# Eight modulation units earlier, another pass order, and a layernorm written out by hand in a two-layer diffusion trunk

## The chip, the cores and the metric

One core of a Trainium2 chip runs the whole program. The metric is the device time of one execution in microseconds; the median of the runs counts. TensorE (PE) does the matrix products, VectorE (DVE), ScalarE (ACT) and GpSimd (POOL) the elementwise work, and SyncE's queue (SP) issues the loads.

## The reference

A latent stream x of 512 tokens and 1024 features goes through two layers, with 256 context tokens beside it that the first layer's attention reads. Layer 0 mixes by grouped attention of 16 heads over 4 key and value heads, layer 1 by a Conformer convolution module, and each ends with a squared-ReLU feed-forward stage of 4096. All of it is in 32 bit floats.

```python
sh1, sc1, g1, sh2, sc2, g2 = split(silu(c) @ mod_w[i] + mod_b[i], 6)     # modulation of layer i
h = rms_norm(x, norm1_g[i]) * (1 + sc1) + sh1
y = dense_gqa(h, hc) if i == 0 else conformer_conv(h)
x = x + g1 * y
h = rms_norm(x, norm2_g[i]) * (1 + sc2) + sh2
x = x + g2 * (square(relu(h @ mlp_up[i])) @ mlp_down[i])

def conformer_conv(h):
    a, g = split(h @ w_pw1 + b_pw1, 2)
    u = a * sigmoid(g)
    u = depthwise_conv(u, w_dw, width=31) + b_dw
    u = silu(layer_norm(u, ln_g, ln_b))          # over the 1024 channels
    return u @ w_pw2 + b_pw2
```

## The kernel before

Features lie on the 128 partitions, in eight tiles of 128 x 512 (`x[j]`, the normed activations as high part `hh[j]` and low part `hl[j]`). A product of 32 bit floats is made of three matmuls: high weights by high activations, high weights by low activations, low weights by high activations (`passes`). Weights come in 1 MB loads (`raw`, two buffers). ACT casts the high part `whi` and DVE subtracts the low part `wlo` (`split_parts`, L418 and L423), in halves of 128 x 1024; for positions in `POOLW`, numbers of the list of weight loads, POOL subtracts. The pool for these parts is `whl`, or, for the up pairs of the later feed-forward stage, `extra[0]` (four buffers each).

The six modulation vectors of a layer are needed as columns. DVE makes them in 80 units (`mod_unit`, L654): one multiplies a load of 512 KB (`mraw`, two buffers) by a row and adds it up. `mod_run(k)` does the next k units and issues the load for two units ahead on SP, so a unit's load waits until the unit two places earlier is done. Units are strewn over the program as filling work: one or two in each head of the attention, `WOT` many around the halves of the projection behind it, eight behind the first up product of the feed-forward stage, more between its later products.

`pair_gemm` makes four output tiles in four PSUM banks, in two halves of 256 columns, `hf`. It is used in `proj_residual` (the attention's output and the convolution's second product, both with an evacuation on DVE for each bank and half that adds to x and takes the squares for the next norm), for the first up product, and for the first pointwise product of the convolution. `mlp` is the feed-forward stage: `relu2` squares on ACT (L705, L691, L692, the high part `ah`) and subtracts on DVE (L697, the low part `al`), then down products alternate with up products. At the end of layer 0's stage the last down product goes in two halves (L912) with the norm for layer 1 between them.

`conv(j)` makes the depthwise convolution of tile j as matmuls, evacuates it in 16 pieces of 32 x 128 (L1599 on ACT, L1596 on DVE), and `center` (L1619 to L1627) subtracts or adds an offset, squares on ACT and adds into the sums `ds_` and `qs`. Behind tile 7 two matmuls for each half sum over the partitions (L1673, L1674), ACT and DVE form the inverse deviation (`r0`), and for each tile DVE subtracts and scales (L1693, L1694), ACT applies silu and casts the high part (L1696, L1697), and POOL subtracts the low part `hl` (L1698). ACT's functions lie in tables that `act_set` loads (L390).

Outside of blocks named `manual_schedule`, the order on each engine is set by the framework's scheduler, which moves instructions past each other where data allow; inside them it is the order in which the code is written.

## Time and profile before

| | |
|---|---|
| median of three runs | 1283.16 us (1281.66 to 1286.63) |
| profiled execution | 1286.02 us, of which the span is 1284.0 |
| PE busy | 1227.1 us (96%) |
| DVE, ACT, POOL busy | 946.5 (74%), 693.7 (54%), 123.0 (10%) |
| chain that ended last | PE 78%, DVE 11%, issue 4%, ACT 4%, DMA 3% |
| granted clock, mean | 0.98 |

Matmuls overlap, so a busy PE is one that has a matmul under way. A row of the timeline gives the start, the time of its instructions together, engine, line, operation and tiles, and in brackets the idle time ahead of it on that engine with the instruction that ended it. The chain is followed back from the last instruction to whatever released it.

### The profile page before, as it was taken

What the parts mean: (1) busy time and instruction counts of PE and PEld (TensorE: products, weight loads), DVE (VectorE), ACT (ScalarE), POOL (GpSimd) and SP (SyncE); (2) the same over time, 40 slices, a digit from 0 to 9 for tenths busy, and PEclk for the clock granted to TensorE, in tenths of its full rate; (3) what the DMA queues carried; (4) which work ended last, traced back from release to release, by engine and by line L of the source; (5) the groups of instructions that cost most, each with busy time, mean ns of one, the idle gap of its engine ahead of it and who ended that gap; (6) DMA issues with size and microseconds to landing.
All of it is one profiled execution on the core that took longest, in us unless ns stands there. A gap on an engine that the chain in (4) does not pass through costs nothing.

```text
span 1284.0 us, 18207 instructions
## 1 busy us (share of the span) xinstructions
PE 1227.1 (96%) x6964; PEld 1042.8 (81%) x6964; DVE 946.5 (74%) x1665; ACT 693.7 (54%) x1297; POOL 123.0 (10%) x172
## 2 busy tenths in 40 slices
...
GB/s 347 158 70 85 31 63 66 67 97 108 217 115 267 180 214 163 164 181 128 168 148 148 165 133 172 181 124 1 132 67 66 91 107 99 99 99 100 102 96 65
DMA packets 36086, 163.08 MB, mean 127 GB/s; under 512 B 4000, under 2 KB 4384, under 8 KB 25120
## 3 DMA queue, kind: packets, MB, share of 16 engines
...
q8 instruction: 54, 0.88, 0.3%
...
## 4 chain that ended last, share of the span: by engine, by line
PE 78%; DVE 11%; issue 4%; ACT 4%; DMA 3%; POOL 0%; SPq 0%; DVEq 0%; ACTq 0%; POOLq 0%
PE sn L750 16%; PE mm L629 9%; PE mm L630 9%; PE mm L631 9%; PE pv L630 7%; PE pv L631 6%; PE pv L629 6%; PE pv L1429 4%; PE pv L1588 2%; PE sn L1369 2%; PE mm L1411 1%; PE mm L1410 1%; DVE wlo L423 1%; DMA mraw<-in_modt_dram 1%; DVE mlo L1015 1%
## 5 line engine op out<-in xcount | busy, mean ns | idle before, releaser
L418 ACT CAST whi<-raw 128x1024 fp32r<-128x1024 f32 x128 | 132.7, 1050 | 170.2 <-PE mm L630 62.0
L423 DVE TENSOR_TENSOR wlo<-raw,whi 128x1024 fp32r<-128x1024 f32 x124 | 150.8, 1223 | 56.0 <-ACT whi L418 53.4
L629 PE MATMUL mm<-hh,whi 128*128 128x256 f32 (+1 forms) x408 | 133.9, 329 | 0.0
L630 PE MATMUL mm<-hl,whi 128*128 128x256 f32 (+1 forms) x408 | 132.9, 326 | 0.0
L631 PE MATMUL mm<-hh,wlo 128*128 128x256 f32 (+1 forms) x408 | 132.9, 327 | 0.0
L629 PE MATMUL mm<-ah,whi 128*128 128x512 f32 (+1 forms) x324 | 123.0, 380 | 3.1 <-DVE x L912 3.1
L630 PE MATMUL mm<-al,whi 128*128 128x512 f32 (+1 forms) x324 | 123.1, 380 | 0.0
L631 PE MATMUL mm<-ah,wlo 128*128 128x512 f32 (+1 forms) x324 | 123.1, 380 | 0.0
L654 DVE SCALAR_TENSOR_TENSOR t<-mraw,sbc 128x1024 bf16<-128x1024 f32 x80 | 97.4, 1222 | 17.4 <-DMA mraw<-in_modt_dram 17.2
L454 DVE TENSOR_TENSOR wlo<-raw,whi 128x1024 fp32r<-128x1024 f32 (+1 forms) x80 | 86.9, 1087 | 12.5 <-ACT whi L446 12.3
L446 ACT CAST whi<-raw 128x1024 fp32r<-128x1024 f32 (+1 forms) x80 | 75.2, 941 | 34.7 <-DMA raw<-in_up_dram 15.6
L629 PE MATMUL pv<-hh,whi 128*128 128x256 f32 (+1 forms) x264 | 84.6, 321 | 9.7 <-ACT hh L1697 4.3
L750 PE MATMUL sn<-hh,wlo 128*128 128x256 f32 x320 | 89.7, 280 | 0.0
L750 PE MATMUL sn<-hl,whi 128*128 128x256 f32 x320 | 89.7, 280 | 0.0
L630 PE MATMUL pv<-al,whi 128*128 128x512 f32 (+1 forms) x224 | 86.1, 384 | 3.8 <-DVE al L697 3.8
L750 PE MATMUL sn<-hh,whi 128*128 128x256 f32 x320 | 89.6, 280 | 0.0
L797 DVE SCALAR_TENSOR_TENSOR x<-mm,mcol,x 128x512 f32<-128x512 f32 x65 | 48.7, 750 | 50.5 <-PE mm L631 50.5
L631 PE MATMUL pv<-ah,wlo 128*128 128x512 f32 (+1 forms) x224 | 85.7, 383 | 0.0
L629 PE MATMUL pv<-ah,whi 128*128 128x512 f32 (+1 forms) x224 | 85.6, 382 | 0.0
L630 PE MATMUL pv<-hl,whi 128*128 128x256 f32 (+1 forms) x264 | 84.2, 319 | 0.9 <-POOL hl L1698 0.9
L631 PE MATMUL pv<-hh,wlo 128*128 128x256 f32 (+1 forms) x264 | 84.3, 319 | 0.6 <-POOL wlo L423 0.6
L629 PEld LDWEIGHTS mm<-hh,whi 128*128 128x128 f32 x408 | 78.1, 192 | 7.3 <-ACT t L1641 0.4
...
## 6 DMA issues: line engine op xcount, KB each, us to landing
mraw<-in_modt_dram SPq DMA_DIRECT2D x80, 512.0 KB, 4.5
...
mraw<-in_modp_dram SPq DMA_DIRECT2D x10, 512.0 KB, 8.4
...
```

The source lines that it names most:

```text
L418: nc.scalar.copy(hi, raw[:, i * 1024:(i + 1) * 1024])
L423: eng.tensor_tensor(out=lo, in0=raw[:, i * 1024:(i + 1) * 1024], in1=hi.bitcast(F32), op=ALU.subtract)
L446: nc.scalar.copy(hi[:, :n], raw[:, o:o + n])
L454: nc.vector.tensor_tensor(out=lo[:, :n], in0=raw[:, o:o + n], in1=hi[:, :n].bitcast(F32), op=ALU.subtract)
L629: nc.tensor.matmul(acc, lhsT=ahi, rhs=bhi, start=first, stop=False)
L630: nc.tensor.matmul(acc, lhsT=ahi, rhs=blo, start=False, stop=False)
L631: nc.tensor.matmul(acc, lhsT=alo, rhs=bhi, start=False, stop=last)
L654: nc.vector.scalar_tensor_tensor(out=tmp(1024, mybir.dt.bfloat16), in0=raw, scalar=1.0, in1=sbc, op0=ALU.mult, op1=ALU.mult, accum_out=mco ...
L750: nc.tensor.matmul(acc, lhsT=a, rhs=b, start=first and k == 0 and i == 0, stop=k == 3 and i == 2, skip_group_check=not first)
L797: nc.vector.scalar_tensor_tensor(out=x[j], in0=acc, scalar=col(l, 5, j), in1=x[j], op0=ALU.mult, op1=ALU.add)
L1369: nc.tensor.matmul(sn[:, :384], lhsT=q1[:, tt * P:(tt + 1) * P], rhs=k1[kv][:, b * 384:(b + 1) * 384], start=True, stop=True)
L1429: nc.tensor.matmul(pv, lhsT=vt[:, f, i:i + P], rhs=p_, start=t == 0, stop=t == NKT - 1)
```

## The change

Six things are changed.

- `POOLW` is empty: the low parts of the second and third pointwise weight loads go from POOL to DVE.
- `WOT` becomes ((4, 4, 2), (3, 0, 0)), and the last three heads of the attention do a unit each; `mod_run(8)` behind the first up product is gone. So eight of the 80 units move: three into the attention, five into the projection.
- The last two down weights of layer 0 are split into the pool of the up pairs instead of `whl`.
- `pair_gemm` goes, for each k, through four matmuls of high by high, four of low weights, and four of low activations, instead of three for each bank in turn.
- The last two tiles of the convolution are evacuated half by DVE and half by ACT from two banks (`MERGED`); the table load for Ln and Exp moves to just behind the last sigmoid; the last tile enters the sums by matmuls that accumulate onto those of `ds_` and `qs`, without additions on DVE.
- The layernorm is written in a `manual_schedule` of DVE and ACT, in which scaling and subtracting alternate by tile and silu and cast too, and both halves' deviations are formed ahead of the silu table load.

```diff
--- before.py
+++ after.py
@@ -33,15 +33,15 @@
 NBLK = 7
 SHUF = 2
 OFFJ = 6
-LASTD = 3
+MERGED = {6: 2, 7: 2}
 KVCUT = [2, 3, 4]
 NU = 16
 KP = (0, 3)
 QP = (1, 0)
 RM = ((1, 1), (1, 1))
 SPLIT = (3,)
-POOLW = (43, 44)
-WOT = ((4, 4, 0), (0, 0, 0))
+POOLW = ()
+WOT = ((4, 4, 2), (3, 0, 0))
 FULL = [t for t in range(NKT) if t not in SPLIT]
 
 B0 = 1
@@ -504,7 +504,7 @@
                 wlist.append(up[l, g])
             else:
                 wlist.append(down[l, g, i[0]])
-        mlp_pos.append((start, set(ups)))
+        mlp_pos.append((start, set(ups + ([len(wlist) - 2, len(wlist) - 1] if l == 0 else []))))
 
     mlp_w(0)
     for i in range(8):
@@ -607,9 +607,14 @@
         for hf in range(2):
             hs = HS[hf]
             for k in range(NT):
-                for i in range(4):
-                    passes(accs[i][:, hs], *ws[i // 2](k * 256 + i % 2 * P, P), hh[k][:, hs], hl[k][:, hs],
-                           k == 0, k == NT - 1)
+                ops = [(accs[i][:, hs], *ws[i // 2](k * 256 + i % 2 * P, P)) for i in range(4)]
+                bhi, blo = hh[k][:, hs], hl[k][:, hs]
+                for acc, wh, _ in ops:
+                    nc.tensor.matmul(acc, lhsT=wh, rhs=bhi, start=k == 0, stop=False)
+                for acc, _, wl in ops:
+                    nc.tensor.matmul(acc, lhsT=wl, rhs=bhi, start=False, stop=False)
+                for acc, wh, _ in ops:
+                    nc.tensor.matmul(acc, lhsT=wh, rhs=blo, start=False, stop=k == NT - 1)
             if evac is not None:
                 for i in range(4):
                     evac(i, hf, accs[i][:, hs])
@@ -761,8 +766,6 @@
             extra[0], extra[1] = mp, ups
             proj_residual(l, v, norm_mlp(l, full))
             accs = pair_gemm(None, None)
-            if l == 0:
-                mod_run(8)
             for i in range(4):
                 relu2(mp, at, i, accs[i])
             t, quad, t1_split = quads(mp, full)
@@ -1502,7 +1505,7 @@
                 while tasks.get(g):
                     tasks[g].pop(0)()
                 if t == 2 and h < NH:
-                    mod_run(2 if h % 4 == 0 and h < 12 else 1 if h < 13 else 0)
+                    mod_run(2 if h % 4 == 0 and h < 12 else 1)
                 if g == NH * NKT - 12:
                     w_prefetch(1)
 
@@ -1573,8 +1576,8 @@
             cv = ps.tile([P, 512], F32, tag="pv", name="pv", bufs=2)
             last = j == NT - 1
             cvs = [cv] * NPH
-            if last:
-                cvs[LASTD:] = [mm_bank()] * (NPH - LASTD)
+            if j in MERGED:
+                cvs[MERGED[j]:] = [ps.tile([P, 512], F32, tag="mm", name="mm", bufs=3)] * (NPH - MERGED[j])
             zj = cp.tile([P, SEQ], F32, name=f"z{j}")
             off = None
             if j >= OFFJ:
@@ -1588,11 +1591,17 @@
                     nc.tensor.matmul(cvs[gq][:, gq * P:(gq + 1) * P], lhsT=tz[:, b], rhs=u[:, gq, b + B0:b + B0 + P],
                                      start=b == b0, stop=b == NBLK - 1)
             z.append(zj)
+            if last:
+                md.extend(sn_bank()[:, 0:256] for _ in range(2))
+                eq.extend((sn_bank()[:, 0:256], ps.tile([P, 512], F32, tag="mm", name="mm", bufs=3)[:, 0:256]))
+                for hf in range(2):
+                    nc.tensor.matmul(md[hf], lhsT=inv_d, rhs=ds_[:, HS[hf]], start=True, stop=False)
+                    nc.tensor.matmul(eq[hf], lhsT=inv_d, rhs=qs[:, HS[hf]], start=True, stop=False)
             for s in range(NPH):
                 for gq in range(4):
                     ch = slice(gq * 32, (gq + 1) * 32)
                     dst, src = zj[ch, s * P:(s + 1) * P], cvs[gq][s * 32:(s + 1) * 32, gq * P:(gq + 1) * P]
-                    if last and gq < LASTD:
+                    if gq < MERGED.get(j, 0):
                         nc.vector.scalar_tensor_tensor(out=dst, in0=src, scalar=pcol("bdw", j)[ch],
                                                        in1=off[ch, s * P:(s + 1) * P], op0=ALU.add, op1=ALU.add)
                     else:
@@ -1615,17 +1624,21 @@
             if off is None:
                 nc.vector.tensor_tensor(out=z[j][:, hs], in0=z[j][:, hs], in1=cb[:, hs], op=ALU.subtract)
             else:
-                ch = slice(LASTD * 32 if j == NT - 1 else 0, P)
+                ch = slice(MERGED[j] * 32, P)
                 nc.vector.tensor_tensor(out=z[j][ch, hs], in0=z[j][ch, hs], in1=off[ch, hs], op=ALU.add)
             s = tmp(256)
             nc.scalar.activation(s, z[j][:, hs], AF.Square)
             if j == 0:
                 nc.vector.tensor_copy(qs[:, hs], s)
                 nc.vector.tensor_copy(ds_[:, hs], z[j][:, hs])
+            elif j == NT - 1:
+                nc.tensor.matmul(md[hf], lhsT=inv_d, rhs=z[j][:, hs], start=False, stop=True)
+                nc.tensor.matmul(eq[hf], lhsT=inv_d, rhs=s, start=False, stop=True)
             else:
                 nc.vector.tensor_tensor(out=ds_[:, hs], in0=ds_[:, hs], in1=z[j][:, hs], op=ALU.add)
                 nc.vector.tensor_tensor(out=qs[:, hs], in0=qs[:, hs], in1=s, op=ALU.add)
 
+        md, eq = [], []
         for j in range(NT):
             if j == 0:
                 accs4 = pair_gemm(None, None)
@@ -1639,6 +1652,8 @@
                         passes(accs[m], *w(k * 256 + m * P, P), hh[k], hl[k], k == 0, k == NT - 1)
             sg = tmp()
             nc.scalar.activation(sg, accs[1], AF.Sigmoid, bias=pcol("bpw1", 8 + j))
+            if j == NT - 1:
+                act_set("natural_log_exp_and_others")
             u = cp.tile([P, 4, P + 8], F32, tag="u", name="u", bufs=3)
             nc.gpsimd.memset(u[:, :, 0:4], 0.0)
             nc.gpsimd.memset(u[:, :, P + 4:], 0.0)
@@ -1664,38 +1679,57 @@
                     center(i // 2, i % 2)
             if j:
                 conv(j - 1)
-        act_set("natural_log_exp_and_others")
         conv(NT - 1)
-        md, eq = sn_bank(), sn_bank()
-        rs = [None, None]
-        for hf in range(2):
+        var = [cp.tile([P, 256], F32, name=f"var{hf}") for hf in range(2)]
+        r0 = [cp.tile([P, 256], F32, name=f"r0_{hf}") for hf in range(2)]
+        ET = mybir.EngineType
+
+        def ln_var(hf):
             hs = HS[hf]
-            nc.tensor.matmul(md[:, hs], lhsT=inv_d, rhs=ds_[:, hs], start=True, stop=True)
-            nc.tensor.matmul(eq[:, hs], lhsT=inv_d, rhs=qs[:, hs], start=True, stop=True)
             m2 = tmp(256)
-            nc.scalar.activation(m2, md[:, hs], AF.Square)
-            var = cp.tile([P, 256], F32, name=f"var{hf}")
-            nc.vector.scalar_tensor_tensor(out=var, in0=eq[:, hs], scalar=EPS, in1=m2, op0=ALU.add, op1=ALU.subtract)
-            r0 = cp.tile([P, 256], F32, name=f"r0_{hf}")
-            nc.scalar.activation(r0, var, AF.Ln)
-            nc.scalar.activation(r0, r0, AF.Exp, scale=-0.5)
-            rs[hf] = (var, r0)
-        act_set("silu_and_others")
-        for hf in range(2):
+            nc.scalar.activation(m2, md[hf], AF.Square)
+            nc.vector.scalar_tensor_tensor(out=var[hf], in0=eq[hf], scalar=EPS, in1=m2, op0=ALU.add, op1=ALU.subtract)
+            nc.scalar.activation(r0[hf], var[hf], AF.Ln)
+            nc.scalar.activation(r0[hf], r0[hf], AF.Exp, scale=-0.5)
+
+        def ln_sub(hf, j):
+            n = z[j][:, HS[hf]]
+            nc.vector.tensor_tensor(out=n, in0=n, in1=md[hf], op=ALU.subtract)
+
+        def ln_rstd(hf):
+            t = tmp(256)
+            nc.vector.tensor_tensor(out=t, in0=r0[hf], in1=r0[hf], op=ALU.mult)
+            nc.vector.tensor_tensor(out=t, in0=t, in1=var[hf], op=ALU.mult)
+            nc.vector.scalar_tensor_tensor(out=r0[hf], in0=t, scalar=-3.0, in1=r0[hf], op0=ALU.add, op1=ALU.mult)
+
+        def ln_out(hf, j):
             hs = HS[hf]
-            var, r0 = rs[hf]
-            t = tmp(256)
-            nc.vector.tensor_tensor(out=t, in0=r0, in1=r0, op=ALU.mult)
-            nc.vector.tensor_tensor(out=t, in0=t, in1=var, op=ALU.mult)
-            nc.vector.scalar_tensor_tensor(out=r0, in0=t, scalar=-3.0, in1=r0, op0=ALU.add, op1=ALU.mult)
+            n = z[j][:, hs]
+            nc.vector.scalar_tensor_tensor(out=n, in0=n, scalar=-0.5, in1=r0[hf], op0=ALU.mult, op1=ALU.mult)
+            v = tmp(256)
+            nc.scalar.activation(v, n, AF.Silu, bias=pcol("lnb", j), scale=pcol("lng", j))
+            nc.scalar.copy(hh[j][:, hs], v)
+            nc.gpsimd.tensor_tensor(out=hl[j][:, hs], in0=v, in1=hh[j][:, hs].bitcast(F32), op=ALU.subtract)
+
+        with tc.manual_schedule(engines={ET.DVE, ET.Activation}):
+            ln_var(0)
+            for j in range(3):
+                ln_sub(0, j)
+            ln_var(1)
+            act_set("silu_and_others")
+            ln_rstd(0)
             for j in range(NT):
...
+                ln_out(0, j)
+                if j + 3 < NT:
+                    ln_sub(0, j + 3)
+                else:
+                    ln_sub(1, j + 3 - NT)
+                if j == NT - 1:
+                    ln_rstd(1)
+            for j in range(NT):
+                ln_out(1, j)
+                if j + 3 < NT:
+                    ln_sub(1, j + 3)
         act_set("natural_log_exp_and_others")
     mlp(1, 2, None)
```

The order of the instructions moves beyond the lines of the diff, since the scheduler places them. Three places are shown, each before and after. (Line numbers differ by three to five from one kernel to the other.)

The first place is the end of the attention on DVE: behind the second to last head's `hl_199` up to the last head's `hl_201`. `mraw` marks modulation units, `phl` the probabilities' low part, `dn`, `rd` and `ou` the division of a head's output. Before:

```order
L1469 TENSOR_TENSOR hl_199<-ou,hh_198 128x512
L423 TENSOR_TENSOR wlo<-raw,whi 128x1024
L1422 TENSOR_TENSOR phl<-pp,phl 128x512
L423 TENSOR_TENSOR wlo<-raw,whi 128x1024
L1459 TENSOR_TENSOR dn<-dn,rd 128x512
L1460 SCALAR_TENSOR_TENSOR rd<-dn,rd 128x512
L1463 SCALAR_TENSOR_TENSOR ou<-ou,rd 128x512
L1469 TENSOR_TENSOR hl_201<-ou,hh_200 128x512
```

And after the change:

```order
L1472 TENSOR_TENSOR hl_199<-ou,hh_198 128x512
L659 SCALAR_TENSOR_TENSOR t,mcol<-mraw,sbc 128x1024 x2
L423 TENSOR_TENSOR wlo<-raw,whi 128x1024
L1425 TENSOR_TENSOR phl<-pp,phl 128x512
L659 SCALAR_TENSOR_TENSOR t,mcol<-mraw,sbc 128x1024
L423 TENSOR_TENSOR wlo<-raw,whi 128x1024
L659 SCALAR_TENSOR_TENSOR t,mcol<-mraw,sbc 128x1024 x2
L1462 TENSOR_TENSOR dn<-dn,rd 128x512
L1463 SCALAR_TENSOR_TENSOR rd<-dn,rd 128x512
L1466 SCALAR_TENSOR_TENSOR ou<-ou,rd 128x512
L1472 TENSOR_TENSOR hl_201<-ou,hh_200 128x512
```

Five units stand between the two heads' low parts where none did. Earlier in the attention two units that stood together behind one head are a single one now.

The second place is the start of the first feed-forward stage, from the last norm to the first down product. On DVE, `al` is what the first down product reads. Before:

```order
L423 TENSOR_TENSOR wlo<-raw,whi 128x1024 x2
L654 SCALAR_TENSOR_TENSOR t,mcol<-mraw,sbc 128x1024 x2
L423 TENSOR_TENSOR wlo<-raw,whi 128x1024 x3
L654 SCALAR_TENSOR_TENSOR t,mcol<-mraw,sbc 128x1024 x2
L423 TENSOR_TENSOR wlo<-raw,whi 128x1024
L654 SCALAR_TENSOR_TENSOR t,mcol<-mraw,sbc 128x1024 x2
L663 TENSOR_TENSOR mcol<-mcol,par_t 128x8
L697 TENSOR_TENSOR al<-t,ah 128x512 x4
```

And after:

```order
L423 TENSOR_TENSOR wlo<-raw,whi 128x1024 x2
L702 TENSOR_TENSOR al<-t,ah 128x512 x4
L423 TENSOR_TENSOR wlo<-raw,whi 128x1024 x4
L659 SCALAR_TENSOR_TENSOR t,mcol<-mraw,sbc 128x1024
L702 TENSOR_TENSOR al<-t,ah 128x512
```

No unit stands ahead of the four `al`, and only one pair of low weight parts does; on ACT, in the same place, six casts of weights stood ahead of the four relus (L705) before:

```order
L625 ACTIVATE hh_200<-t,mcol 128x256
L418 CAST whi<-raw 128x1024 x6
L705 ACTIVATE t<-pv 128x512 x2
L691 ACTIVATE t<-t 128x512 x2
L692 CAST ah<-t 128x512 x2
L705 ACTIVATE t<-mm 128x512 x2
```

And after the change:

```order
L630 ACTIVATE hh_200<-t,mcol 128x256
L418 CAST whi<-raw 128x1024 x2
L710 ACTIVATE t<-pv 128x512 x2
L696 ACTIVATE t<-t 128x512 x2
L697 CAST ah<-t 128x512 x2
L710 ACTIVATE t<-mm 128x512 x2
L696 ACTIVATE t<-t 128x512 x2
L697 CAST ah<-t 128x512 x2
L418 CAST whi<-raw 128x1024 x4
```

Four of the six casts come behind the relus.

The third place is the end of layer 0's feed-forward stage on DVE, the evacuations of the last full down products (x from `pv` or `mm`) with the weights for the next products between them. Before:

```order
L797 SCALAR_TENSOR_TENSOR x_3030<-mm,mcol,x_3030 128x512
L423 TENSOR_TENSOR wlo<-raw,whi 128x1024
L797 SCALAR_TENSOR_TENSOR x_3031<-mm,mcol,x_3031 128x512
L797 SCALAR_TENSOR_TENSOR x_3032<-pv,mcol,x_3032 128x512
L423 TENSOR_TENSOR wlo<-raw,whi 128x1024
L797 SCALAR_TENSOR_TENSOR x_3033<-pv,mcol,x_3033 128x512
L697 TENSOR_TENSOR al<-t,ah 128x512
L654 SCALAR_TENSOR_TENSOR t,mcol<-mraw,sbc 128x1024
L423 TENSOR_TENSOR wlo<-raw,whi 128x1024
```

And after:

```order
L800 SCALAR_TENSOR_TENSOR x_3042<-mm,mcol,x_3042 128x512
L423 TENSOR_TENSOR wlo<-raw,whi 128x1024 x3
L800 SCALAR_TENSOR_TENSOR x_3043<-mm,mcol,x_3043 128x512
L800 SCALAR_TENSOR_TENSOR x_3044<-pv,mcol,x_3044 128x512
L423 TENSOR_TENSOR wlo<-raw,whi 128x1024 x2
L800 SCALAR_TENSOR_TENSOR x_3045<-pv,mcol,x_3045 128x512
L702 TENSOR_TENSOR al<-t,ah 128x512
L659 SCALAR_TENSOR_TENSOR t,mcol<-mraw,sbc 128x1024
L423 TENSOR_TENSOR wlo<-raw,whi 128x1024 x2
```

Four more low weight parts stand here. Two of them stood between the scaling and the shifting of tiles in the norm that follows, on DVE, before (the other two were POOL's):

```order
L624 SCALAR_TENSOR_TENSOR t<-x_3028,gcol,sn 128x256
L626 SCALAR_TENSOR_TENSOR hl_187<-t,mcol,hh_186 128x256
L624 SCALAR_TENSOR_TENSOR t<-x_3029,gcol,sn 128x256
L423 TENSOR_TENSOR wlo<-raw,whi 128x1024 x2
L626 SCALAR_TENSOR_TENSOR hl_189<-t,mcol,hh_188 128x256
L626 SCALAR_TENSOR_TENSOR hl_191<-t,mcol,hh_190 128x256
L626 SCALAR_TENSOR_TENSOR hl_193<-t,mcol,hh_192 128x256
```

And after:

```order
L629 SCALAR_TENSOR_TENSOR t<-x_3040,gcol,sn 128x256
L631 SCALAR_TENSOR_TENSOR hl_187<-t,mcol,hh_186 128x256
L631 SCALAR_TENSOR_TENSOR hl_189<-t,mcol,hh_188 128x256
L631 SCALAR_TENSOR_TENSOR hl_191<-t,mcol,hh_190 128x256
L629 SCALAR_TENSOR_TENSOR t<-x_3041,gcol,sn 128x256
L629 SCALAR_TENSOR_TENSOR t<-x_3042,gcol,sn 128x256
```

There are no low weight parts in that place any more.

## Rows read from the trace of the kernel before

**Rows 1.** Timeline of PE, attention and first feed-forward: start, us, instruction, [idle, released by].

```profile
281.55 0.44 PE L1369 MATMUL sn<-k,q 128*128 128x384 f32 x1 [1.32 <-DVE nm L1371]
...
390.62 0.50 PE L629 MATMUL pv<-hh,whi 128*128 128x512 f32 x1 [1.15 <-ACT t L705]
...
400.52 0.80 PE L630 MATMUL pv<-al,whi 128*128 128x512 f32 x1 [3.80 <-DVE al L697]
```

**Rows 2.** Timeline of PE, boundary of the layers.

```profile
720.04 0.38 PE L629 MATMUL mm<-ah,whi 128*128 128x256 f32 x1 [3.07 <-DVE x L912]
...
725.17 0.39 PE L631 MATMUL pv<-hh,wlo 128*128 128x256 f32 x1 [0.63 <-POOL wlo L423]
...
729.59 0.61 PE L565 MATMUL sn<-inv_d,sqa 128*128 128x1 f32 x4 [1.52 <-DVE sqa L589]
```

**Rows 3.** Timeline of PE, end of the convolution and layernorm.

```profile
868.41 1.73 PE L1588 MATMUL mm<-u,tz 128*128 128x128 f32 x14
...
879.15 1.22 PE L1673 MATMUL sn<-ds__7091,inv_d 128*128 128x256 f32 x2 [1.46 <-DVE qs L1627]
...
885.49 0.58 PE L629 MATMUL pv<-hh,whi 128*128 128x256 f32 x1 [4.27 <-ACT hh L1697]
...
887.00 0.58 PE L630 MATMUL pv<-hl,whi 128*128 128x256 f32 x1 [0.92 <-POOL hl L1698]
```

**Rows 4.** Busy time in stretches: length, engines' busy us, clock, DMA.

```profile
320.00:360.00 40.00, 37.88 (x310) 37.01 (x310) 29.25 (x60) 17.84 (x31) 0.00 (x0) 1.00 0.58 196
400.00:440.00 40.00, 39.48 (x163) 31.74 (x164) 29.22 (x42) 12.32 (x17) 0.00 (x0) 0.96 0.61 205
686.00:699.00 13.00, 13.00 (x77) 11.28 (x76) 7.96 (x12) 4.01 (x7) 0.00 (x0) 1.00 0.41 129
720.00:760.00 40.00, 37.81 (x272) 36.00 (x273) 25.95 (x45) 23.90 (x49) 15.65 (x27) 0.91 0.49 177
```

**Rows 5.** Timeline of DVE, attention to first down product.

```profile
302.77 0.69 DVE L1469 TENSOR_TENSOR hl<-ou,hh 128x512 fp32r<-128x512 f32 x1 [0.69 <-ACT hh L1466]
...
313.17 0.69 DVE L1459 TENSOR_TENSOR dn<-dn,rd 128x512 f32<-128x512 f32 x1 [3.03 <-ACT rd L1456]
...
321.05 0.88 DVE L1516 SCALAR_TENSOR_TENSOR x<-mm,mcol,x 128x256 f32<-128x256 f32 x2 [4.35 <-PE mm L631]
...
395.69 1.22 DVE L654 SCALAR_TENSOR_TENSOR t<-mraw,sbc 128x1024 bf16<-128x1024 f32 x1 [2.00 <-DMA mraw<-in_modt_dram]
```

**Rows 6.** Loads between 250 and 300 us: count, KB, median us to landing.

```profile
mraw<-in_modt_dram SPq DMA_DIRECT2D x7, 512.0 KB, 3.6
```

**Rows 7.** Loads of the whole kernel, the same columns.

```profile
mraw<-in_modt_dram SPq DMA_DIRECT2D x80, 512.0 KB, 4.5
```

**Rows 8.** Timeline of DVE, boundary of the layers.

```profile
713.08 2.36 DVE L423 TENSOR_TENSOR wlo<-raw,whi 128x1024 fp32r<-128x1024 f32 x2
...
723.42 6.11 DVE L589 TENSOR_TENSOR sqa<-sqa,t 128x256 f32<-128x256 f32 x5 [0.42 <-ACT t L584]
```

**Rows 9.** Timeline of POOL, boundary of the layers and layernorm.

```profile
722.76 4.90 POOL L423 TENSOR_TENSOR wlo<-raw,whi 128x1024 fp32r<-128x1024 f32 x2
...
885.58 6.72 POOL L1698 TENSOR_TENSOR hl<-t,hh 128x256 fp32r<-128x256 f32 x7 [20.03 <-issue]
```

**Rows 10.** Timeline of ACT, end of the convolution.

```profile
862.35 2.47 ACT L1652 COPY u<-ug 32x128 f32<-32x128 f32 x8 [1.31 <-DVE ug L1646]
...
864.84 5.96 ACT L1599 ACTIVATE z<-pv,par_t 32x128 f32<-32x128 f32 x16
...
871.73 1.28 ACT L390 ACT_TABLE_LOAD   x1
...
873.02 1.48 ACT L1599 ACTIVATE z<-mm,par_t 32x128 f32<-32x128 f32 x4
...
874.89 0.42 ACT L1621 ACTIVATE t<-z 128x256 f32<-128x256 f32 x1 [0.38 <-DVE z L1619]
```

**Rows 11.** Timeline of DVE, layernorm.

```profile
885.59 0.76 DVE L1694 SCALAR_TENSOR_TENSOR z<-z,r 128x256 f32<-128x256 f32 x2
```

7 lines of the change are left out of this document (removed).

## The prediction

> **What bounds the kernel now.** I read the head of the page first: TensorE is busy nearly all the time, so only what it waits, and the stretches at the lower of its two clock levels (1.2 instead of 2.4 GHz), are to be had. Then I went through the timeline of PE for the stretches that the diff touches and took the bracketed wait ahead of each row; each such wait is time that passes on PE. There are three clusters. In the attention and the first feed-forward stage [rows 1] PE waits 1.32 us at 281.55, 1.15 at 390.62 and 3.80 at 400.52, the last for the low parts `al` of the activations. Between the two layers [rows 2] it waits 3.07, 0.63 and 1.52 us. Behind the convolution [rows 3] it has nothing between 870.1 (868.41 + 1.73) and 885.49 but eight small matmuls for the layernorm sums, and then waits 0.92 more. The granted clock of 0.96 over 400 to 440 and 0.91 over 720 to 760 [rows 4] says that about 3.2 us (0.04 x 40 / 0.5) and 7.2 us there ran at the lower level, which costs half of that, 1.6 and 3.6 us; in both stretches the fall follows the long wait.
>
> **Term 1, the eight moved units.** Ahead of the first down products DVE runs modulation units, and each waits for its own load: 2.00 us at 395.69 [rows 5], and the next one again. The four `al` are queued behind them, and PE behind those. In the new order no unit stands between the low weight parts and `al`, and on ACT the four relus come ahead of the casts of the next down weight, so I take the waits at 390.62 and 400.52 and the clock loss behind them as gone: 1.15 + 3.80 + 1.6 = 6.5 us. In the attention two units that stood on either side of a row-maximum come later, and I take the wait of 1.32 as gone.
>
> Against it stand the units' new places. Three go into the last heads, where DVE was idle for 3.03 us ahead of the final division at 313.17 [rows 5]. There five units now stand between the last two heads' `hl`, the first behind the `hl` that ends at 303.5 (302.77 + 0.69), the last ahead of that division. With two buffers a load can only start when the unit two places earlier is done, so the third unit's load starts at 304.8 and the fifth's when the third is done. With 3.6 us for a load, as in the attention [rows 6], and 1.3 for a unit, the fifth ends at 304.8 + 3.6 + 1.3 + 3.6 + 1.3 = 314.6, 1.4 us behind the division's old start. The last head comes that much later, and so do the eight loads of x, which are queued on SP behind the same loads. Bounds: nothing, if the loads get ahead earlier, and 3.2, with the 4.5 us of the whole kernel's median [rows 7] twice. The other five, at 1.3 us each with the accumulator read, put 6.5 us on DVE in the projection, where it has 40 - 29.25 = 10.75 us free [rows 4]. They delay the norm and the evacuations that stand behind them; between nothing and 6.5 I take 1.5, since the free time is spread over the stage. Sum of term 1: -6.5 - 1.3 + 1.4 + 1.5 = -4.9.
>
> **Term 2, the pass order of the four-bank product.** It issues the same number of matmuls. What changes is that the four banks end within the last four matmuls of a half instead of three apart. A half's evacuation costs 0.48 us, then 0.40 for each that follows (0.88 for two [rows 5]), and the next half needs the banks at once. The order of PE shows that the next half's starts on the four banks were set 4 matmuls, about 0.5 us, apart, which covers a bank's 0.40 nearly; what is left is the first evacuation, 0.45 us longer than before at each of four such boundaries (two in the attention's projection, two in the convolution's second), 1.8 us in all. Bounds: nothing, and four times 1.4, if all four evacuations (0.48 + 3 x 0.40 = 1.68) are waited for and only the end of the matmuls ahead covers 0.3.
>
> **Term 3, the layer boundary.** The wait of 3.07 at 720.04 is for an evacuation that is queued on DVE behind modulate steps and 2.36 us of `wlo` at 713.08 [rows 8]. The two `wlo` leave this place in the new order, because the weights of the first pointwise product are split earlier (the last two down weights no longer hold their buffers): four more `wlo`, 4.9 us at 1.22 each, now stand in 686 to 699, where DVE is busy for only 7.96 of 13 us [rows 4], so they just fit. The wait of 0.63 is for a low weight part on POOL, and 1.52 is for the sums of squares: five of them took 6.11 us at 723.42 [rows 8], 1.22 each, while POOL worked on `wlo` from 722.76 for 4.90 us [rows 9]. With POOL emptied both go. Sum of the waits 5.22, and of the clock's 3.6 half, since parts of it may hang on smaller waits that stay: 1.8. On the other side, `al` of the last down product now stands behind two `wlo` that may wait for a load, for which I allow 0.8 us, two thirds of one `wlo`, and what is left of POOL's four parts on DVE later fits into its 40 - 25.95 us [rows 4]. Sum -6.2. Bounds: -3, if only the first wait goes; -8.5, if all the clock comes back.
>
> Of this the Trainium skill, "SBUF — State Buffer", section "Who interferes with whom", says that a DVE instruction with two SBUF inputs and a GpSimd instruction that reads SBUF lock each other out for a whole instruction. The stretched sums agree with it. The same rule speaks against term 4, see the rivals.
>
> **Term 4, the layernorm.** Before, the evacuation of the seventh block takes ACT 5.96 us for 16 pieces, 0.37 each, from 864.84 [rows 10], DVE waits for it, then a table load of 1.28 us stands at 871.73, and the last sums enter PE at 879.15. Now both last blocks are divided evenly, the table load sits in the idle 1.31 us at 862.35, and the last block goes into the sums by accumulating matmuls, without the adds. From the last convolution matmul at 870.1: 8 x 0.37 = 3.0 us of evacuation, 0.42 for the square (as at 874.89) and about the same for the add ahead of it [rows 10] make 874.0. From the entry of the last sums to the first matmul of the product it took 885.49 - 879.15 = 6.34 us; the same operations follow now, so the product starts at 880.4, 5.1 us earlier. The 0.92 us for the first `hl` go too, because low parts are needed only after eight matmuls. Sum -6.0; the stretch at the lower clock behind it I leave as it is. Bounds: -3 (the second half of the sums does not overlap) and -7.5.
>
> The Trainium skill, "ScalarE: Activation LUTs", section "What ACT_TABLE_LOAD costs", puts a drain of 1.38 us behind each load, 2.66 in all. Here the next activation starts at 873.02, right where the load ends [rows 10], so the row decides; by the page the moved load would overrun its gap by 1.35 us and the term would be -4.6, an estimate.
>
> **The sum.** -4.9 + 1.8 - 6.2 - 6.0 = -15.3 us. The profiled execution took 1286.0 us (a span of 1284.0 and 2.0 around it), 2.9 above the median of 1283.2. So 1270.7 for a run like the profiled one, and 1268 at the median.
>
> **Rivals.** (a) *The moved units only move the wait.* Loads of 4.5 us through two buffers run at one unit in about 2.9 us, and five units in the projection plus three in the last heads hold up the x evacuations as they held `al`. For it: a unit waited 2.0 us for its load where several came close together [rows 5]. Against it: DVE's free 10.75 us. Term 1 is then zero: 1273.
> (b) *The new pass order waits for all four evacuations* at each boundary, 4 x 1.4 = 5.6 instead of 1.8: 1272. For it: all banks end together; against it: the starts set apart.
> (c) *DVE inherits the contention.* The split moved from POOL to DVE and the early `wlo` delay evacuations of the down products between 686 and 760 as POOL did; only half of term 3 stays: 1271.
> (d) *POOL and DVE lock each other in the layernorm.* POOL makes each `hl` in 0.96 us (6.72 for seven) [rows 9], and the scaling on DVE has two SBUF inputs. If each waits for a whole POOL step, a tile costs DVE 0.96 and two steps of 0.38, 1.72 us, where PE needs 12 x 37.88 / 310 = 1.47 us for its twelve matmuls [rows 4]; over sixteen tiles 4.0 us are lost: 1272. Against it: at 885.59, with POOL at work, two scalings took 0.76 us [rows 11]. The page on SBUF named above would have it so.
> (e) *Slower.* Each of the five units put into the projection stands in DVE's fixed order ahead of an evacuation and is waited for with a whole load of 4.5 us [rows 7] by PE: +22.5 us against the forecast, 1290. It decides against the change from 15.3 / 5 = 3.1 us of PE time for each unit. Against it: the loads are issued two ahead, and the largest wait of a unit in [rows 5] is 2.0.
>
> **How the numbers follow.** Forecast 0.53, (a) 0.14, (b) 0.09, (c) 0.10, (d) 0.04, two of these together 0.05, (e) 0.05. A measurement here can tell about 0.5%, 6.4 us, from no change (the three runs spread by 0.4%). All single rivals but (e) stay below 1276.7; two together come to 1275 to 1277, so most of that counts as no change, with a share of the outer bounds of the others: 0.86 faster, 0.09 the same, 0.05 slower. The range: if all bounds fall well, 7.8 for term 1 with nothing against it, no cost at the boundaries, 8.5 and 7.5 are 23.8 in all, about 1260; if term 1 comes to nothing and term 3 to 3, 7.2 are left, or 1276, and 1 us is added for dearer boundaries. That leaves out (e) and worse pairs.
>
> **What would show it.** Right: no wait for `al` near 400 and no lower clock behind it; sums of squares of 0.4 us each at the layer boundary and no wait above 1 us for an evacuation there; the product behind the convolution starting some 10.3 us after the last convolution matmul instead of 15.4; about 0.5 us more at the four boundaries. Wrong: DVE units with waits for `mraw` ahead of x evacuations between 315 and 370, an x load that lands after 326, or the waits of PE at 716 to 732 standing as they are.

## The result, and the profile after

The changed kernel takes 1269.09 us (median of four runs, 1268.17 to 1270.89), the kernel before beside it 1284.08 (1281.66 to 1286.63): a ratio of 0.988, with an interval of 0.986 to 0.991. The forecast was 1268, the range 1260 to 1277. The profiled execution's span is 1266.3 us instead of 1284.0, 17.7 less.

The head of the page after (busy time, share of the span and instructions of each engine):

```profile
PE 1222.5 (97%) x6972; PEld 1039.8 (82%) x6972; DVE 946.4 (75%) x1669; ACT 692.9 (55%) x1293; POOL 110.8 (9%) x168
```

The work is the same (DVE 946.5 before, 946.4 now). PE's busy time falls by 4.6 us only, since what went is mostly waiting. The busy time of four stretches, in order PE, PEld, DVE, ACT, POOL, then the granted clock, the DMA share and GB/s:

```profile
320.00:360.00 40.00, 36.92 (x297) 35.66 (x296) 32.07 (x64) 13.53 (x25) 0.00 (x0) 1.00 0.72 250
400.00:440.00 40.00, 40.00 (x173) 32.18 (x172) 29.84 (x46) 13.67 (x18) 0.00 (x0) 1.00 0.67 238
686.00:699.00 13.00, 13.00 (x97) 12.36 (x96) 11.87 (x21) 6.46 (x10) 0.00 (x0) 1.00 0.73 253
720.00:760.00 40.00, 39.89 (x292) 37.06 (x291) 24.60 (x44) 28.04 (x58) 5.85 (x18) 1.00 0.49 165
```

Against [rows 4]: DVE is fuller in the projection (320 to 360) and in 686 to 699, where the early `wlo` went and PE still never stops; at the first down products (400 to 440) and the layer boundary (720 to 760) PE runs through and the clock is 1.00 instead of 0.96 and 0.91. The timeline of PE shows where the old waits were and what stands there now:

```profile
319.18 0.39 PE L613 MATMUL mm<-hh,whi 128*128 128x256 f32 x1 [0.29 <-DVE x L1519]
...
322.67 0.38 PE L613 MATMUL pv<-hh,whi 128*128 128x256 f32 x1 [1.19 <-DVE x L1519]
...
344.52 0.39 PE L613 MATMUL pv<-hh,whi 128*128 128x256 f32 x1 [0.23 <-DVE x L1519]
...
348.87 0.39 PE L613 MATMUL mm<-hh,whi 128*128 128x256 f32 x1 [1.58 <-DVE x L1519]
...
362.19 0.38 PE L613 MATMUL pv<-hh,whi 128*128 128x256 f32 x1 [1.78 <-ACT hh L630]
...
712.33 0.38 PE L634 MATMUL mm<-ah,whi 128*128 128x256 f32 x1 [0.19 <-DVE x L915]
...
867.58 0.58 PE L613 MATMUL mm<-hh,whi 128*128 128x256 f32 x1 [5.04 <-ACT hh L1711]
...
882.25 0.36 PE L613 MATMUL mm<-hh,whi 128*128 128x256 f32 x1 [0.32 <-DVE x L1519]
...
905.74 0.39 PE L613 MATMUL mm<-hh,whi 128*128 128x256 f32 x1 [0.23 <-DVE x L1519]
```

The wait for a row maximum and those for `al` near 400 are gone, and so is everything at the layer boundary but 0.19 us. In the projection (319 to 363) there are small waits at the boundaries of its halves and three of 1.2 to 1.8 us, for evacuations of x and for the norm. The kernel before had waits there too, but shorter ones in all:

```profile
324.61 0.39 PE L629 MATMUL pv<-hh,whi 128*128 128x256 f32 x1 [1.26 <-DVE x L1516]
...
347.54 0.39 PE L629 MATMUL pv<-hh,whi 128*128 128x256 f32 x1 [0.87 <-DVE x L1516]
```

Behind the convolution the product waits 5.04 us, and its own boundaries 0.32 and 0.23.

**The stages.** To compare kernels I cut each trace at the same rows of PE, DVE and ACT: the first probability-by-value matmul, the first and last x evacuation of the projection, the first product of an up pair, the first evacuation of the last down product (the one in halves), the first and last matmul of the convolution, and the first matmul and last evacuation of its second product. Each number is the difference of two such starts, in us. "Rest" is from the first of these rows to the end of the span; the unchanged code ahead of it takes 151.0 to 155.3 us in these profiles, so kernels are compared by "rest" below.

| kernel | attention | projection | to up pairs | up pairs | boundary | convolution | layernorm | 2nd product | rest |
|---|---|---|---|---|---|---|---|---|---|
| before | 167.5 | 42.0 | 161.9 | 173.4 | 56.3 | 115.2 | 15.6 | 53.5 | 1130.5 |
| after | 165.8 | 47.0 | 154.4 | 174.4 | 46.9 | 115.2 | 11.0 | 53.8 | 1113.5 |
| after, repeated | 165.8 | 45.2 | 154.4 | 174.3 | 47.0 | 115.2 | 11.0 | 53.5 | 1111.3 |
| units only | 165.8 | 46.5 | 154.5 | 173.5 | 54.5 | 115.1 | 15.6 | 53.3 | 1123.7 |
| after, units back | 168.5 | 39.9 | 161.7 | 174.3 | 47.0 | 115.1 | 11.0 | 52.7 | 1115.2 |
| units one a head | 172.6 | 44.4 | 155.0 | 174.4 | 46.9 | 115.1 | 11.0 | 53.5 | 1117.8 |
| units early | 169.5 | 39.5 | 155.0 | 174.3 | 47.0 | 115.2 | 11.0 | 53.8 | 1110.2 |
| units early, mixed order | 169.5 | 40.1 | 155.0 | 174.2 | 47.1 | 115.2 | 11.0 | 52.8 | 1110.0 |
| order only | 168.2 | 41.0 | 162.0 | 173.4 | 56.0 | 115.2 | 15.6 | 52.6 | 1129.1 |
| after, old order | 165.8 | 49.7 | 155.6 | 174.3 | 47.3 | 114.0 | 11.0 | 52.0 | 1114.7 |
| after, POOL splits | 166.4 | 47.3 | 154.4 | 174.3 | 50.9 | 115.2 | 11.0 | 53.4 | 1117.8 |
| after, old buffers | 166.0 | 46.2 | 154.4 | 173.4 | 53.2 | 115.2 | 11.0 | 53.4 | 1117.7 |
| after, old layernorm | 165.9 | 47.5 | 154.4 | 174.3 | 47.0 | 115.2 | 15.6 | 53.1 | 1117.9 |
| after, plain code order | 165.9 | 47.3 | 154.4 | 174.2 | 47.1 | 115.1 | 11.3 | 53.8 | 1114.1 |

After less before: attention -1.7, projection +5.0, to the up pairs -7.4, boundary with the up pairs -8.5 (the up pairs take 0.9 longer, the boundary 9.4 less), layernorm -4.7, the remaining stages together 0.2 and the start -0.7: -17.7.

### The profile page after: what moved, and what is told of

Read it like the earlier page. It is cut to its first block, busy times and chain, and to the rows that moved or that the text cites. A ratio compares the mean times of both kernels' runs of the same rounds, so it can differ in the third digit from the quotient of the medians.

```text
span 1266.3 us, 18194 instructions
## 1 busy us (share of the span) xinstructions
PE 1222.5 (97%) x6972; PEld 1039.8 (82%) x6972; DVE 946.4 (75%) x1669; ACT 692.9 (55%) x1293; POOL 110.8 (9%) x168
## 4 chain that ended last, share of the span: by engine, by line
PE 77%; DVE 12%; ACT 5%; DMA 4%; issue 2%; POOL 0%; SPq 0%; DVEq 0%; ACTq 0%; POOLq 0%
PE sn L755 16%; PE mm L634 7%; PE mm L636 7%; PE mm L635 7%; PE pv L635 5%; PE pv L636 5%; PE pv L634 5%; PE pv L1432 4%; DMA mraw<-in_modt_dram 2%; PE sn L1372 2%; ACT z L1608 2%; PE mm L613 2%; PE mm L1413 1%; PE mm L1414 1%; DVE wlo L423 1%
## 5 line engine op out<-in xcount | busy, mean ns | idle before, releaser
L418 ACT CAST whi<-raw 128x1024 fp32r<-128x1024 f32 x128 | 132.1, 1049 | 149.0 <-DMA raw<-in_down_dram 47.1
L423 DVE TENSOR_TENSOR wlo<-raw,whi 128x1024 fp32r<-128x1024 f32 x128 | 154.9, 1223 | 43.2 <-ACT whi L418 42.4
L659 DVE SCALAR_TENSOR_TENSOR t<-mraw,sbc 128x1024 bf16<-128x1024 f32 x80 | 97.3, 1220 | 15.6 <-DMA mraw<-in_modt_dram 15.4
L800 DVE SCALAR_TENSOR_TENSOR x<-mm,mcol,x 128x512 f32<-128x512 f32 x66 | 49.3, 749 | 54.7 <-PE mm L636 54.5
L1432 PE MATMUL pv<-pp,vt 128*128 128x512 f32 x160 | 81.6, 591 | 0.0
L1374 DVE TENSOR_REDUCE nm<-sn 128x1 f32<-128x384 f32 x128 | 64.9, 550 | 14.5 <-PE sn L1372 14.2
L636 PEld LDWEIGHTS mm<-ah,wlo 128*128 128x128 f32 x328 | 61.6, 188 | 12.7
L634 PEld LDWEIGHTS mm<-ah,whi 128*128 128x128 f32 x328 | 61.7, 188 | 11.2 <-DVE x L915 0.4
L635 PEld LDWEIGHTS mm<-al,whi 128*128 128x128 f32 x328 | 61.6, 188 | 10.9
L1416 ACT ACTIVATE pp<-mm 128x512 f32<-128x512 f32 x96 | 56.8, 596 | 22.3 <-PE mm L1414 21.8
L613 PE MATMUL mm<-hh,whi 128*128 128x256 f32 x272 | 59.9, 291 | 7.6 <-ACT hh L1711 5.0
```

Source lines behind the costliest of these rows:

```text
L418: nc.scalar.copy(hi, raw[:, i * 1024:(i + 1) * 1024])
L423: eng.tensor_tensor(out=lo, in0=raw[:, i * 1024:(i + 1) * 1024], in1=hi.bitcast(F32), op=ALU.subtract)
L613: nc.tensor.matmul(acc, lhsT=wh, rhs=bhi, start=k == 0, stop=False)
L634: nc.tensor.matmul(acc, lhsT=ahi, rhs=bhi, start=first, stop=False)
L635: nc.tensor.matmul(acc, lhsT=ahi, rhs=blo, start=False, stop=False)
L636: nc.tensor.matmul(acc, lhsT=alo, rhs=bhi, start=False, stop=last)
```

## The experiments

Each ran once, with a profile, but for the mixed order and the repeat of after, which were timed four times, one of them with a profile.

**Where the units' gain goes.** First the units alone, in the kernel before:

```diff
-WOT = ((4, 4, 0), (0, 0, 0))
+WOT = ((4, 4, 2), (3, 0, 0))
...
-            if l == 0:
-                mod_run(8)
...
-                    mod_run(2 if h % 4 == 0 and h < 12 else 1 if h < 13 else 0)
+                    mod_run(2 if h % 4 == 0 and h < 12 else 1)
```

> The kernel before with the eight modulation units moved and nothing else. Prediction's term 1: from the attention to the first up pair 4 to 5 us shorter than before. The theory formed from the run with the units put back: the first feed-forward stage gains 7 us, the attention 1 to 2, the projection loses 5 to 9, so the sum is within 3 us of nothing, and more likely a loss than in the changed kernel, since the old pass order needs the low parts earlier.

It took 1278.62 us, and 6.8 less than before in "rest": -1.7 in the attention, +4.5 in the projection, -7.4 behind it, and -1.8 at the boundary, which it does not touch. At that boundary the waits of [rows 2] are all there (3.06, 1.56 and, at 723.80, 1.52 us), and PE is busy for less of the time, but the granted clock stays at its full level where it fell before. PE's timeline of this run, then the windows around the boundary, of this run and of before:

```profile
714.73 0.38 PE L629 MATMUL mm<-ah,whi 128*128 128x256 f32 x1 [3.06 <-DVE x L910]
...
719.39 0.39 PE L631 MATMUL pv<-hh,wlo 128*128 128x256 f32 x1 [1.56 <-POOL wlo L423]
```

```profile
710.00:740.00 30.00, 23.86 (x192) 22.96 (x191) 25.00 (x54) 18.41 (x35) 6.63 (x10) 1.00 0.54 193
710.00:740.00 30.00, 24.79 (x175) 23.79 (x175) 25.46 (x54) 16.67 (x35) 5.34 (x9) 0.89 0.48 176
```

So these waits don't bring a fall of the clock in every execution; what else decides it no run here shows. The other way round, the same three edits undone in the changed kernel:

> The changed kernel with the eight modulation units back behind the first up product (and none in the last three heads and two fewer places in the projection). Theory: the waits of PE of 1.2 and 3.8 us in the first feed-forward stage and the lower clock behind them return (6.5 us), the waits of 1.6 and 1.8 us late in the projection go (the changed kernel loses 4.5 us more there than before), the row-maximum wait of 1.3 us in the attention returns: 3.5 to 5.5 us longer in all. Rival: the projection's waits come from the pass order and not from the units, so they stay and this run is 7 to 9 us longer.

It took 1269.81. The waits for `al` return in PE's timeline, as in [rows 1]:

```profile
397.08 0.79 PE L635 MATMUL pv<-al,whi 128*128 128x512 f32 x1 [3.21 <-DVE al L702]
```

and in DVE's timeline the load that holds them up:

```profile
393.84 1.23 DVE L659 SCALAR_TENSOR_TENSOR t<-mraw,sbc 128x1024 bf16<-128x1024 f32 x1 [2.90 <-DMA mraw<-in_modt_dram]
```

The stretch to the up pairs costs 7.3 again, but the projection gives 7.1 of it back; the attention takes 2.7 more. That is 2.9 together, under the 3.5 to 5.5 expected, and 1.7 in "rest", because the second product, which these edits don't touch, is 1.1 shorter here. So the units' place was worth 7.4 us where they left, and most of that was paid again where they went. DVE's timeline of the changed kernel shows an evacuation that waits for its load of x, for which PE waits 1.19, and a unit that waits for its own load ahead of an evacuation, for which PE waits 1.58:

```profile
322.13 0.48 DVE L1519 SCALAR_TENSOR_TENSOR x<-pv,mcol,x 128x256 f32<-128x256 f32 x1 [1.48 <-DMA x<-in_xT_dram]
...
347.18 1.23 DVE L659 SCALAR_TENSOR_TENSOR t<-mraw,sbc 128x1024 bf16<-128x1024 f32 x1 [1.94 <-DMA mraw<-in_modt_dram]
348.33 0.48 DVE L1519 SCALAR_TENSOR_TENSOR x<-mm,mcol,x 128x256 f32<-128x256 f32 x1
```

The wait for a load of x is not all payment: before had one of 1.31, behind PE's 1.26 at 324.61. With the units put back, or early as below, there is none. The unit's wait ahead of an evacuation that PE waits for is new.

Could the attention take the five units without a price? One unit a head and a second in every other head, with `WOT` as in the run before:

```diff
-                if t == 2 and h < NH:
-                    mod_run(2 if h % 4 == 0 and h < 12 else 1)
+                if t == 2 and h < NH or t == 5 and h < NH and h % 2 == 0:
+                    mod_run(1)
```

> The changed kernel with the modulation units kept out of the second half of the projection: one unit in each head of the attention, a second one in every other head but at another point of the head, none added in the projection. Theory (the units' wait was only moved into the projection, where they and their loads hold evacuations, the loads of x and the casts): PE's waits there of 1.2, 1.6 and 1.8 us fall away, those in the first feed-forward stage stay away, and the span is 4 to 7 us shorter than the changed kernel's. Rival: the attention pays as much, through waits for row maxima on DVE like the 1.3 us before, and the span is within 2 us of the changed kernel's.

It took 1270.74, and the attention 172.6 us, 6.8 more than in after. The place in the head matters: behind the last block of keys (`t == 5`) the unit stands ahead of row maxima, and PE waits for one in six such heads, 0.64 to 0.85 us each (the longest, from PE's timeline):

```profile
201.07 0.44 PE L1372 MATMUL sn<-k,q 128*128 128x384 f32 x1 [0.85 <-DVE nm L1374]
```

So the two units of a head went back to the old place, in the first twelve heads:

```diff
-WOT = ((4, 4, 2), (3, 0, 0))
+WOT = ((0, 4, 0), (0, 0, 0))
...
-                    mod_run(2 if h % 4 == 0 and h < 12 else 1)
+                    mod_run(2 if h < 12 else 1)
```

> The changed kernel with 28 of the first 32 modulation units in the attention (two together in each of the first twelve heads, at the point where heads had two before) and the last four in the first half of the projection, so none in the tail of the attention and none in the second half. Theory: two units at this point of a head cost the attention about 0.2 us (the heads with two before took 19.86 us a pair of heads instead of 19.66), 2 us in all; the projection takes 40 to 42 us between first and last evacuation instead of 47; the first feed-forward stage keeps its gain. Span from the sixth head pair's division on as in the changed kernel minus 5, in all 2 to 5 us shorter. Rival: the projection's length does not hang on the units but on when the loads of x and of the weights land, and stays at 46 to 47 us.

It took 1265.86. The projection fell to 39.5, the attention cost 3.7 more (PE waits 0.31 to 0.70 us for `phl` in five heads in which after has no such wait), and "rest" is 1110.2 against 1113.5 and 1111.3 of the two executions of after. PE's waits at the projection's boundary are the small ones alone:

```profile
323.68 0.38 PE L613 MATMUL mm<-hh,whi 128*128 128x256 f32 x1 [0.29 <-DVE x L1519]
...
347.19 0.39 PE L613 MATMUL pv<-hh,whi 128*128 128x256 f32 x1 [0.23 <-DVE x L1519]
```

**The pass order.** Undone in the changed kernel:

```diff
-                for acc, wh, _ in ops:
-                    nc.tensor.matmul(acc, lhsT=wh, rhs=bhi, start=k == 0, stop=False)
-                for acc, _, wl in ops:
-                    nc.tensor.matmul(acc, lhsT=wl, rhs=bhi, start=False, stop=False)
-                for acc, wh, _ in ops:
-                    nc.tensor.matmul(acc, lhsT=wh, rhs=blo, start=False, stop=k == NT - 1)
+                for i in range(4):
+                    passes(accs[i][:, hs], *ws[i // 2](k * 256 + i % 2 * P, P), hh[k][:, hs], hl[k][:, hs],
+                           k == 0, k == NT - 1)
```

> The changed kernel with the old pass order of the four-bank product (three passes of one bank, then the next). Theory of the prediction: the new order costs about 0.45 us at each of four half boundaries, so this run is 1 to 2 us shorter than the changed kernel's span of 1266.3 us, and nothing else moves. Rival: the new order pays for itself, because the low parts of weights and activations are needed later; then PE waits for low parts come back (behind the layernorm 0.9 us, at the layer boundary 0.6 us) and the span is equal or up to 2 us longer.

It took 1271.10, 1.2 more in "rest": the convolution and its second product are 1.2 and 1.8 faster without the new order, the projection 2.6 and the stretch to the up pairs 1.2 slower. The 1.2 in the convolution is a wait of PE for POOL's sum `zsum`. PE's timeline of after, then of this run:

```profile
806.56 1.13 PE L1676 MATMUL sn<-zsum,inv_h 128*128 128x512 f32 x2 [1.56 <-POOL zsum L1617]
```

```profile
810.40 1.13 PE L1671 MATMUL sn<-zsum,inv_h 128*128 128x512 f32 x2 [0.34 <-POOL zsum L1612]
```

The first pointwise product, ahead of the convolution, is a four-bank product too; why POOL's sum comes later behind the new order was not tried. Of the 1.8 in the second product, 1.1 lie ahead of its first boundary: from its first matmul to its second half it takes 13.57 us here and 14.67 in after, but 13.57 also with the new order in the run with the units put back, so this part is not the order's. What stays is the boundary between its two rounds of four banks: the third of its four quarters takes 11.5 us here and in the mixed version below, 12.0 to 12.3 with the new order. And the new order alone, put into the kernel before (the same edit the other way):

> The kernel before with the new pass order of the four-bank product and nothing else. The prediction's term: 0.45 us more at each of four half boundaries, 1.8 us longer than before. The theory formed from the runs so far: the projection takes about 2 us less (39.9 us between its first and last evacuation as in the run with the units put back, against 42.0), because the low parts of weights and activations are needed four to eight matmuls later; the wait for a low part on POOL at the layer boundary (0.6 us) goes; the two halves of the convolution's second product take 1 to 2 us more; in all 0 to 2 us shorter than before.

It took 1285.20 beside 1284.12 of before. In "rest" it gains 1.4: 1.0 in the projection and 0.9 in the second product, where the wait of 0.92 for the first `hl` [rows 3] is gone, less 0.8 in the attention, which it does not touch. At the boundaries of the second product, where before has no wait, PE's timeline has two:

```profile
898.96 0.35 PE L613 MATMUL pv<-hh,whi 128*128 128x256 f32 x1 [0.32 <-DVE x L1521]
...
922.67 0.39 PE L613 MATMUL mm<-hh,whi 128*128 128x256 f32 x1 [0.44 <-DVE x L1521]
```

PE's wait for `zsum` is 1.57 here and 0.45 before, but the convolution takes 115.2 in both: over 820 to 840 the granted clock was 1.00 here and 0.91 before. So the order costs something at the boundaries and ahead of `zsum`, and at the start of the second product it gets some back, because low parts are wanted later. All these amounts are about one or two us, which is what one projection varies between executions of the same code (47.0 and 45.2). To see whether one can have both, units early and the old order in the convolution's second product alone:

```diff
+                if banks_first:
+                    for i in range(4):
+                        passes(accs[i][:, hs], *ws[i // 2](k * 256 + i % 2 * P, P), hh[k][:, hs], hl[k][:, hs],
+                               k == 0, k == NT - 1)
+                    continue
...
-            pair_gemm(evac, (lambda hf: after(sq, hf)) if half else None, WOT[half] if l == 0 else (0, 0, 0))
+            pair_gemm(evac, (lambda hf: after(sq, hf)) if half else None, WOT[half] if l == 0 else (0, 0, 0), l == 1)
```

> The same units as in the run before, and the old pass order in the convolution's second product alone, where putting the old order back had shortened the two halves by 1.1 and 0.7 us. Theory: another 1 to 2 us, together 4 to 7 us shorter than the changed kernel. Rival: the 1.8 us were the phase in which the lower clock ends and not the boundaries; then nothing is added.

Beside it the changed kernel once more:

> The changed kernel itself again, for comparison on the same chip: 1266 to 1271 us. If the start of the program (before the attention) varies by 1 to 3 us from one execution to the next, as the profiles so far suggest, this profile's span differs from 1266.3 by that much, and the lengths of the later stages by less than 0.7 us each.

The mixed version took 1266.48 (1264.95 to 1269.54; ratio to before 0.987, 0.985 to 0.989), the changed kernel 1267.12 (1265.47 to 1268.24; 0.988, 0.986 to 0.989). The second product is 0.7 to 1.0 shorter, but the two versions can't be told apart by time, and next to the run before the mixed order adds nothing in "rest" (1110.0 and 1110.2). The stages of the two executions of after agree within 0.3 us but for the projection, which differs by 1.9 where under 0.7 was expected. I found none that measurably beats the change.

**The layer boundary.** POOL gets its two weights back:

```diff
-POOLW = ()
+POOLW = (43, 44)
```

> The changed kernel with the four low weight parts of the second and third pointwise loads back on POOL. Theory: the stretched sums of squares (1.2 us each instead of 0.4) and the wait for POOL's low part return, with a lower granted clock after them, 3 to 5 us, all between the last down product and the first convolution. Rival: it was the earlier split of the first pointwise weights alone that removed the waits, and POOL's work, now at another moment, costs under 1 us.

It took 1273.29, and the boundary 4.0 us more. POOL now does its work earlier, since the weights are free earlier. Its timeline, then DVE's, then PE's:

```profile
692.39 2.56 POOL L423 TENSOR_TENSOR wlo<-raw,whi 128x1024 fp32r<-128x1024 f32 x1 [532.62 <-ACT whi L418]
694.91 3.38 POOL L423 TENSOR_TENSOR wlo<-raw,whi 128x1024 fp32r<-128x1024 f32 x1
```

```profile
692.60 3.43 DVE L659 SCALAR_TENSOR_TENSOR t<-mraw,sbc 128x1024 bf16<-128x1024 f32 x1
...
696.92 1.52 DVE L587 COPY sqa<-t 128x256 f32<-128x256 f32 x1
```

```profile
706.50 0.61 PE L565 MATMUL sn<-inv_d,sqa 128*128 128x1 f32 x4 [2.49 <-DVE sqa L589]
```

While POOL subtracts, a modulation unit takes 3.43 instead of 1.22 us and a copy 1.52 instead of 0.28, and PE waits 2.49 for the sums. The sums behind that are unstretched (0.42), as they are in after, where DVE's timeline has:

```profile
716.62 0.42 DVE L589 TENSOR_TENSOR sqa<-sqa,t 128x256 f32<-128x256 f32 x1
```

How the slow ones come about shows in [rows 8] and [rows 9] when their rows are taken one by one. POOL's two parts in the kernel before, then the first two of DVE's five sums of squares:

```profile
722.76 2.36 POOL L423 TENSOR_TENSOR wlo<-raw,whi 128x1024 fp32r<-128x1024 f32 x1
725.09 2.57 POOL L423 TENSOR_TENSOR wlo<-raw,whi 128x1024 fp32r<-128x1024 f32 x1
```

```profile
723.42 1.98 DVE L589 TENSOR_TENSOR sqa<-sqa,t 128x256 f32<-128x256 f32 x1 [0.42 <-ACT t L584]
...
725.51 2.44 DVE L589 TENSOR_TENSOR sqa<-sqa,t 128x256 f32<-128x256 f32 x1
```

The five were not all stretched to 1.22 us: the two that started beside a part of POOL ended 0.3 us after that part (725.40 and 727.95, against 725.12 and 727.66), and the other three took 0.42 to 0.43. In the run with POOL's weights back the unit ends 1.1 us after POOL's first part, the second part, begun beside the unit, takes 3.38 instead of 2.4 to 2.6, and the copy ends 0.15 after that. So the slow sums of [rows 8] were POOL's doing, and one DVE instruction waits for one of POOL's. The Trainium skill, "SBUF — State Buffer", section "Who interferes with whom", has it that a DVE instruction with two SBUF inputs and a reading GpSimd lock each other out; the unit's 3.43 us and the two sums agree. Next, the two down weights back in `whl`:

```diff
-        mlp_pos.append((start, set(ups + ([len(wlist) - 2, len(wlist) - 1] if l == 0 else []))))
+        mlp_pos.append((start, set(ups)))
```

> The changed kernel with the last two down weights split into the same pool as before instead of the up pairs' buffers. Theory: the low parts of the first pointwise weights fall behind the first half of the norm again, the evacuation ahead of the second half waits, and the layer boundary is 3 to 5 us longer (a wait of PE of about 3 us ahead of the second half of the last down product). Rival: without POOL's part DVE takes these low parts without a wait of PE, and the difference is under 1 us.

It took 1274.92: 6.3 more at the boundary, 0.9 less in the up pairs. PE's timeline and the window around it show the old wait, and the lower clock with it:

```profile
716.95 0.58 PE L634 MATMUL mm<-ah,whi 128*128 128x256 f32 x1 [3.06 <-DVE x L915]
```

```profile
714.00:724.00 10.00, 7.05 (x37) 7.05 (x38) 9.19 (x21) 6.37 (x13) 0.48 (x7) 0.66 0.54 190
```

The granted clock of 0.66 over these 10 us lies between the two levels (1.2 and 2.4 GHz); in after it is 1.00 from 720 on, with PE busy for 39.89 of 40 us. The two undone parts cost 4.0 and 5.3 us, 9.3 together, where both at once had brought 8.5: each is needed. In both, the cost is the wait (2.49, and 3.06) and a stretch at a lower clock with it (0.86 over 700 to 710 with POOL's weights back).

**The layernorm.** The convolution's end as before, all else changed (in its core):

```diff
-MERGED = {6: 2, 7: 2}
+LASTD = 3
...
-                nc.tensor.matmul(md[hf], lhsT=inv_d, rhs=z[j][:, hs], start=False, stop=True)
-                nc.tensor.matmul(eq[hf], lhsT=inv_d, rhs=s, start=False, stop=True)
...
+        act_set("natural_log_exp_and_others")
         conv(NT - 1)
...
-        with tc.manual_schedule(engines={ET.DVE, ET.Activation}):
```

> The changed kernel with the whole end of the convolution as before (evacuation of the last two tiles, table load, sums and layernorm). Theory: from the last convolution matmul to the first matmul of the second product 15.4 to 15.7 us instead of 10.9, 4.5 to 6 us longer, and the rest unchanged. Rival: with the new pass order the product can start before the low parts are there, so part of the gain is the pass order's, and undoing the end costs under 4 us.

It took 1273.67, with the layernorm at 15.6 as before. PE's timeline has the old waits:

```profile
863.74 1.22 PE L1676 MATMUL sn<-ds__7091,inv_d 128*128 128x256 f32 x2 [5.47 <-DVE ds__7091 L1629]
...
873.61 0.80 PE L613 MATMUL pv<-hh,whi 128*128 128x256 f32 x2 [4.26 <-ACT hh L1700]
```

Then only the hand order taken out, with the divided evacuations and the accumulating matmuls kept:

```diff
-        with tc.manual_schedule(engines={ET.DVE, ET.Activation}):
-            ln_var(0)
...
+        for hf in range(2):
+            ln_var(hf)
+        act_set("silu_and_others")
+        for hf in range(2):
+            ln_rstd(hf)
             for j in range(NT):
...
+                ln_sub(hf, j)
+                ln_out(hf, j)
```

> The changed kernel with the layernorm's operations in the old order (both halves' deviations, table load, then for each tile subtract, scale, silu, cast, the order left to the scheduler); evacuation, accumulation in matmuls and the moved table load stay. Theory: the gain of 4.7 us comes from the evacuation and the accumulation, which end the sums 5 us earlier; this run is 0 to 1.5 us longer than the changed kernel. Rival: the order by hand is what matters, and this run is 3 to 5 us longer.

It took 1267.90 and the layernorm 11.3 us. The order written out by hand is worth 0.3 us; the other 4.3 come from the divided evacuation, the moved table load and the matmul sums, which no run takes apart. PE's and ACT's timelines of after show what is left of it:

```profile
853.58 3.29 PE L1591 MATMUL mm<-u,tz 128*128 128x128 f32 x28
...
860.10 0.70 PE L1635 MATMUL sn<-z,inv_d 128*128 128x256 f32 x2 [1.50 <-DVE z L1628]
861.39 0.70 PE L1635 MATMUL sn<-z,inv_d 128*128 128x256 f32 x2
```

```profile
847.79 1.28 ACT L390 ACT_TABLE_LOAD   x1
849.08 2.46 ACT L1667 COPY u<-ug 32x128 f32<-32x128 f32 x8
...
856.91 2.59 ACT L1608 ACTIVATE z<-mm,par_t 32x128 f32<-32x128 f32 x7 [0.89 <-PE mm L1591]
860.08 0.42 ACT L1630 ACTIVATE t<-z 128x256 f32<-128x256 f32 x1 [0.58 <-DVE z L1628]
860.52 0.36 ACT L1608 ACTIVATE z<-mm,par_t 32x128 f32<-32x128 f32 x1
...
865.19 1.28 ACT L390 ACT_TABLE_LOAD   x1
866.49 0.60 ACT L1710 ACTIVATE t<-z,par_t 128x256 f32<-128x256 f32 x1
```

## Why the prediction came out right, step by step

The sum was -15.3; the medians differ by 15.0 and the spans by 17.7. The four terms measured one by one come to -19.2, and "rest" fell by 17.0: terms 2 and 3 came out 3.2 and 2.3 us better than forecast, term 4 came out 1.3 worse. That the median fits the sum within 0.3 us is luck; that the waits of terms 1, 3 and 4 went where forecast is not.

**Term 1, forecast -4.9, measured -4.6** (units only: -1.7, +4.5 and -7.4), and -2.9 in after (undone there, the same stages give 2.7, -7.1 and 7.3). The sum holds, its parts don't. The gain at the first down products was 7.4 where I had 6.5. The attention, which I had at +0.1 (1.4 less 1.3), gained 1.7: the wait of 1.32 went, and one of 0.33 with it, and the delay of 1.4 in the last heads did not come. The projection cost three times the 1.5 that I chose between 0 and 6.5: "the free time is spread over the stage" was the step that failed. Free time of DVE is no cover for a unit that waits for its own load, because what stands behind it waits too (1.94 us ahead of the evacuation at 348.33). That is the first of the signs that I had named for being wrong, and it is there. Rival (a), that the units only move the wait, holds for most of it: in after, 5.0 of 7.4 are given back in the projection. With the units early, out of the projection, it is 39.5 us, and the attention pays 3.7 for them instead.

**Term 2, forecast +1.8, measured -1.4** (order alone) and about -1.2 (undone in after): not the way that was forecast. The four boundaries cost about what I took, or less: PE waits 0.29 and 0.23 in the projection with the units early, 0.32 and 0.23 in the convolution's second product of after, 1.07 in brackets against 1.8. In the projection even the old order had waits for evacuations (1.26 and 0.87), which I had passed over. Longer waits in the projection of after stand behind a late unit or load, so rival (b) did not come. What I left out is the rest of what the order does: it needs the low parts of activations later, and I had counted that only once, as the 0.92 us in term 4; and it makes PE wait 1.2 us longer for `zsum` in the convolution. That the low parts are also what saves 1.0 in the projection is argued, not shown. These amounts lie near what executions of the same code differ by, so the sign of the term stays open.

**Term 3, forecast -6.2, measured -8.5,** my bound for the case that all the clock comes back. The waits went as forecast: the four early `wlo` fit (DVE 11.87 of 13 us, PE 13.00), the wait of 3.07 left 0.19, no sum takes more than 0.43 us, and the 0.8 us allowed on the other side is nearly the 0.9 by which the up pairs grow, which goes again when the old buffers return. One reading was wrong: the 1.22 us was a mean over five sums, of which two waited for POOL and three did not. The part mis-sized is the clock: with no wait left it stays at its full level, and there were no "smaller waits that stay" to hold half of it. But it also stayed there in the units-only run, with all the waits, so the 3.6 us are not a sure price of these waits. Rival (c) did not come; PE never stopped between 686 and 699.

**Term 4, forecast -6.0, measured -4.7.** From the last convolution matmul (853.58 + 3.29 = 856.87) to the entry of the last sums at 861.39 it took 4.5 us where I had 3.9, and from there to the product at 867.58 6.2 where I had 6.3: a start 10.7 us behind, not 10.3. The evacuation itself was as quick as forecast (seven pieces in 2.59 us). The failed step is the one behind it, where I put one add and one square: ACT's eighth piece stands at 860.52, behind the square of the first half (860.08), and the second half's add, square and sums behind that, a detour of about 1.0 us (860.52 less 856.91 + 2.59). The 0.92 for `hl` did go, but in the balance of term 2 (the second product is no shorter in after: 53.8 and 53.5 against 53.5). The table load fits its gap: 847.79 + 1.28 = 849.07, and ACT's next instruction starts at 849.08; behind the load at 865.19 the first silu starts at 866.49. So no drain of the 1.38 us given in the Trainium skill, "ScalarE: Activation LUTs", section "What ACT_TABLE_LOAD costs", is seen. Rival (d) did not come as a loss: the scalings take 0.62 to 0.97 us beside POOL's 0.73 to 1.03 for an `hl` in DVE's and POOL's timelines instead of 0.42, but the subtractions of the mean, with an input in PSUM, run beside POOL at 0.41. So a tile takes DVE 0.9 us there (868.23 to 869.12), not the rival's 1.72, and PE waits for none of it between 867.58 and 882.25.

```profile
868.23 0.63 DVE L1708 SCALAR_TENSOR_TENSOR z<-z,r 128x256 f32<-128x256 f32 x1
868.78 0.41 DVE L1697 TENSOR_TENSOR z<-z,sn 128x256 f32<-128x256 f32 x1
869.12 0.62 DVE L1708 SCALAR_TENSOR_TENSOR z<-z,r 128x256 f32<-128x256 f32 x1
```

```profile
871.36 0.74 POOL L1712 TENSOR_TENSOR hl<-t,hh 128x256 fp32r<-128x256 f32 x1 [0.16 <-ACT hh L1711]
```

**Open.** The projection takes 46.5 us with the old pass order and the moved units in one kernel and 49.7 in another, whose code up to there differs in nothing that I can name; each is one execution. Part of it is a load of x: in the slower one DVE waits 2.37 us for it at 322.89 and PE 2.23 behind that, in the other DVE waits 0.52 and 0.81 and PE 1.31 in three pieces. Why it lands later there was not tried. So the sizes of terms 1 and 2 hold to about 2 us. What makes the clock fall at the layer boundary in some executions, and not in the units-only run, is open too.
